# Weight buffers at multiples of 512 bytes, and the first modulation's weights loaded in two halves of the columns

## The chip, the cores and the metric

One core of a Trainium2 chip runs one program. The metric is the device time of one execution in microseconds; for the kernel before it is the median of three runs. The engines are called by the profile's names: PE is TensorE, DVE VectorE, ACT ScalarE, POOL GpSimd, and SP the engine that issues most DMAs. Each runs its own instructions in order.

## The reference

Two layers of a transformer-like block over 256 latent tokens (`x`) and 256 context tokens (`ctx`), width 1024, all in float32. A layer begins with an adaptive norm, whose shift and scale come from a conditioning vector (`c` for the latents, `c_ctx` for the context) through a 1024 x 6144 matrix:

```python
sh1, sc1, g1, sh2, sc2, g2 = split(silu(c) @ w_mod[l] + b_mod[l], 6)
h = layer_norm0(x) * (1.0 + sc1) + sh1
z = h @ w_in + b_in
```

From `z` three mixers are computed (grouped-query attention, a gated linear attention, a neighbourhood attention), gated, summed and projected; then a norm, a second modulation, and a mixture of 32 experts (the top group, then two experts in it), each expert with three matrices of 1024 x 512 (6.3 MB together). The result is the latent stream after two layers.

## The kernel before, in words

`run` (L1645) does, for each layer: the first modulation and norm, the gated linear attention (`gla_gates`, `gla_pair`), attention, neighbourhood attention, merge, output norm, routing, and the experts. Instructions are written in that order and a scheduler places them, by a simulated time line, into each engine's in-order stream; a DMA that is written to `nc.sync` stands in SP's queue, one written to `nc.scalar` in ACT's.

**The start of layer 0.** `setup` (L413) loads the constants (L434). `run` loads four tiles of x, 128 tokens x 1024 columns, 512 KB each, on SP (L1659). `vectors(0)` (L570) loads five small tensors (`bt`, `qk`, `cs`, `wg`, `gn`) and computes the twelve products of the rope table and a few scaled copies on DVE; `setup2` (L441) loads and casts two masks by way of `raw` tiles. Then comes `modulation(0, [0], ...)` (L471): it loads `cT` (L476), computes its SiLU into `sT`, and loads the columns of shift and scale (2048 of the 6144) in 16 tiles `wmod` of 128 x 1024, for each of eight k tiles the two halves of the columns (L493). For every k tile four matmuls with `sT` (32 columns wide, in four column groups of TensorE) add to one PSUM tile, 128 x 512 (L495); an fp32 matmul is two instructions in the profile. So no column is complete until the sixteenth tile has come. The bias `bm` is added (L500), four transposes (L503) and four copies (L517) make `mT`, which holds shift and scale with the feature on the partition. Twelve of the sixteen tiles take buffers of tags that are free at the time (`h4`, `y4`); the last four take the four buffers of tag `raw`, which the first projection weights use next.

**`norm_T`** (L532) computes the statistics of the four x tiles on DVE and the normalised tiles `xh` on ACT (L549). Then come eight parts, (kk, s) for kk = 0 to 3 and s = 0, 1: a part is two k tiles (256 features) of 256 tokens. TensorE transposes (L560), DVE (L565) and ACT (L563) scale and shift one k tile each, ACT casts the result to the rounded high half `hThi` (L291) and DVE or POOL, in turns, subtracts for the low half `hTlo` (L292). Projections are three matmuls per k tile (L380 to L382): high by high, low by high, high by low.

**After it** `gla_gates` (L607) loads `wa`, splits it on ACT and DVE, and accumulates `aT` over k = 0 to 7; the bias on ACT, the gate products `z` (L630), and `projT` (L384) follow, each weight piece coming by way of a `raw` tile (512 KB, L373), a cast on ACT and a subtraction on DVE.

**Where the weights lie.** Pools of SBUF are stacked from the left in the order in which they are opened, some from the right. The staging pool `wp` (`raw`, `whi`, `wlo`, `h4`: 18 tiles of 4 KB per partition) begins 128 bytes past a multiple of 512; the pools opened from the left behind it (`mg`, and for the experts `eg`) begin 64 past one, those from the right (`mp`, `pre`, `ep`) 480 past one. Four two-element tiles `sum0` to `sum3` stand in the pool `lp` ahead of `wp` and take 32 bytes each.

**The experts.** `load` hands out the buffers of the expert weights in rotation: six of the left pool (tag `ew`, 8 KB per partition, 1 MB), then spare staging tiles in pairs (two of 4 KB, 512 KB each), then the right pool's (`ewb`, 8 KB, and the one `pre` buffer of layer 0). The loads stand in SP's queue in that order (L1487), so that in the stream a run of left loads, a run of spare ones and a run of right ones take turns.

Of the kernel before, what the change touches and what calls it, by code (L numbers as in the profile page):

```python
# [10 lines left out]
F32 = mybir.dt.float32  # L11
# [4 lines left out]
AF = mybir.ActivationFunctionType  # L16
ALU = mybir.AluOpType
# [4 lines left out]
NL = 2  # L22
NE = 32
EPS = 1e-6
ALPHA = (2 * NL) ** 0.25
BIG = 1.0e30


A_Q, A_K, B_Q, B_K, B_V, B_R, B_A, C_Q, C_K, C_V, GATE = 0, 512, 768, 1024, 1280, 1792, 2304, 2336, 2848, 3360, 3872
# [135 lines left out]
def _layout(inp):  # L165
# [7 lines left out]

    wm = g["w_mod"].reshape(NL, 8, 128, 3, 2, 1024)
    o["wmod"] = np.ascontiguousarray(wm.transpose(0, 3, 1, 4, 2, 5))
    bm = g["b_mod"].reshape(NL, 3, 4, 512)
    bb = np.zeros((NL, 4, 32, 3, 512), f32)
    bb[:, :, 0] = bm.transpose(0, 2, 1, 3)
# [71 lines left out]
class _Prog:  # L250
# [133 lines left out]
    def projT(self, l, n, ntok):  # L384

        hi, lo = self.piece(l, n)
        p = self.ps("pT")
        for k in range(8):
            s = slice(128 * k, 128 * k + 128)
            self.mm3(p[:, :ntok], hi[:, s], lo[:, s], self.hT(0, k)[:, :ntok], self.hT(1, k)[:, :ntok], k == 0, k == 7)  # L390
        return p

    def projM(self, l, names, kper, width, tiles, sub=None):
# [74 lines left out]
        self.tc.cur_priority -= n  # L468


    def modulation(self, l, groups, tag="raw", tag2="b2", ps="mod"):  # L471

        nc = self.nc
        if l == 0 and 0 in groups:
            cT = self.lp.tile([128, 16], F32, name="cT")
            nc.sync.dma_start(cT, self.a["cT"])  # L476
            th = self.small(16)
            nc.scalar.activation(th, cT, AF.Tanh, scale=0.5)
            sil = self.small(16)
            nc.vector.scalar_tensor_tensor(sil, th, 1.0, cT, op0=ALU.add, op1=ALU.mult)  # L480
            self.sT = self.cp.tile([128, 8, 32], F32, name="sT")
            nc.vector.memset(self.sT, 0.0)
            nc.vector.tensor_scalar(self.sT[:, :, 0:2], sil.rearrange("p (k s) -> p k s", s=2), 0.5, None, op0=ALU.mult)
        for g in groups:
            p = self.ps(ps)
            for k in range(8):
# [42 lines left out]
            self.nc.sync.dma_start(r[:, 512 * i:512 * i + 512], self.md[l, g][row:row + 1, :].to_broadcast([128, 512]))  # L529
        return r  # L530

    def norm_T(self, l, xs):  # L532

        nc = self.nc
        xh = []
# [14 lines left out]
                xh.append(h)  # L550
        hs = [self.t([128, 2, 512], "g4", name="h") for _ in range(4)]
        self.hTt = tuple([self.t([128, 2, 512], "h4", F32R, n) for _ in range(4)] for n in ("hThi", "hTlo"))
        parts = [(s, kk) for s in range(2) for kk in range(4)] if l else [(s, kk) for kk in range(4) for s in range(2)]
        for i, (s, kk) in enumerate(parts):
            ss = slice(256 * s, 256 * s + 256)
            p = self.ps("hT").rearrange("p (k t) -> p k t", k=2)
            for k in range(2):
                kt = 2 * kk + k
                for t in range(2):
                    nc.tensor.transpose(p[:, k, 128 * t:128 * t + 128], xh[2 * s + t][:, 128 * kt:128 * kt + 128], self.ident)  # L560
                sc, sh = (self.mT[l][:, j, s, kt:kt + 1] for j in range(2))
                if k:
                    nc.scalar.activation(hs[kk][:, k, ss], p[:, k], AF.Identity, bias=sh, scale=sc)  # L563
                else:
                    nc.vector.tensor_scalar(hs[kk][:, k, ss], p[:, k], sc, sh, op0=ALU.mult, op1=ALU.add)  # L565
            hi, lo = (self.hTt[j][kk][:, :, ss] for j in range(2))
            self.split(hs[kk][:, :, ss], hi, lo, nc.gpsimd if (kk if l else i) % 2 == PP else None)
# [39 lines left out]
    def gla_gates(self, l):  # L607

        nc = self.nc
        raw = self.raw(l)  # L610
        (nc.scalar if l else nc.sync).dma_start(raw[:, :256], self.a["wa"][l])
        hi, lo = self.t([128, 1024], "whi", F32R), self.t([128, 1024], "wlo", F32R)
        self.split(raw[:, :256], hi[:, :256], lo[:, :256])
        p = self.ps("aT")
        for k in range(8):
            s = slice(32 * k, 32 * k + 32)
            self.mm3(p[:32, :], hi[:, s], lo[:, s], self.hT(0, k), self.hT(1, k), k == 0, k == 7)
        aT = self.t([33, 512], "u2", name="aT")
        nc.scalar.activation(aT[0:32], p[:32], AF.Identity, bias=self.bt[0:32, BT["a"]:BT["a"] + 1])
        nc.vector.memset(aT[32:33], 1.0)  # L620
        self.aT = aT
# [1022 lines left out]
    def run(self):  # L1644
        nc, a = self.nc, self.a  # L1645
        self.md, self.mT, self.mT2, self.nraw = {}, {}, {}, {}
        self.setup()
        self.rp = self.ctx.enter_context(self.tc.tile_pool(name="rp", bufs=1))
        self.x2 = [self.dr.tile([128, 1024], F32, name=f"x2_{t}") for t in range(2)]
        src = [a["x"][0:128], a["x"][128:256], a["cx"][0:128], a["cx"][128:256]]  # L1650
        xs = None
        for l in range(NL):
            T = 4 if l == 0 else 2
            if l == 0:
                left, right = self.mixers(0)
                xs = []
                for t in range(4):
                    x = self.t([128, 1024], "o4", name="x")
                    nc.sync.dma_start(x, src[t])  # L1659
                    xs.append(x)  # L1660
                self.vectors(l)
                self.setup2()
                self.modulation(0, [0], ["h4"] * 8 + ["y4"] * 4 + ["raw"] * 4)
            self.norm_T(l, xs)
            if l:
                self.modulation(1, [1], "o4", "b2", "tmod")
            if l:
# [30 lines left out]
            right.close()  # L1698
            right = self.open("ep", "right", [("ewb", RNG[l]), ("e8", 2), ("g2", T // 2), ("oh", 1), ("o1", 1), ("e2", NE2[l]), *([("c2", NC2[l])] if l else []), ("ct", NCT[l]), ("row", 2)])

            self.sums = [self.cp1(f"sum{t}", 2) for t in range(T)]
            self.experts(l, T)
            if l:
                lgb = self.final_loads(l)
# [38 lines left out]
```

## Time and profile before

| | us |
|---|---|
| median of 3 runs | 2134.95 (2132.41 to 2136.12) |
| profiled execution | 2129.76 |
| its span | 2128.0 |

The span is the time from the first to the last instruction of the profiled execution; what lies around it is 1.76 us. Times in the rows below are microseconds from the span's start. A timeline row is: start, duration, engine, line, operation, tile written <- tiles read, with the idle time of the engine ahead of it and what ended that in brackets; "x4" merges four of a kind. PEclk is the share of TensorE's clock that was granted, DMA share the busy share of the core's 16 DMA engines.

### The profile page before, as it was taken

Reading aid. Unit: us, or ns where it says so; the run is one execution under the profiler, and the core shown is the slowest. Engines: PE = TensorE matmul, PEld = TensorE weight load, DVE = VectorE, ACT = ScalarE, POOL = GpSimd, SP = SyncE. Lnnn points to the kernel's source line nnn. Section 1 sums busy time; section 2 is a strip of 40 time slices with the busy share of each in tenths; the row PEclk is TensorE's granted clock in tenths of the full one; section 3 lists DMA queues with packets and bytes.
Section 4 is the critical chain, followed back from the end, with each engine's and each line's share of the span. In section 5 each row is a group of like instructions: output and inputs, shape, how many; then the busy total and the mean of one; then the engine's idle time right before and its main releaser. Section 6 shows DMA issues by size and latency. Waiting matters only on the chain. (4 is left out here: it accounts for less than half of the span.)

```text
span 2128.0 us, 28181 instructions
## 1 busy us (share of the span) xinstructions
PE 1964.5 (92%) x10749; PEld 1183.4 (56%) x10749; DVE 956.0 (45%) x2275; ACT 569.4 (27%) x1008; POOL 259.9 (12%) x259
## 2 busy tenths in 40 slices
PE   5999999999998998999899698999996999999986
PEld 1676777777885352545253275977895443343332
DVE  4676766464387130222122765776557122222113
ACT  3443344343233000000000454444452101100001
POOL 1322100011110010111011122100020000000000
PEclk9999999999999999999999898999997999999998
DMA  7436222223329899999998734533476999999996
GB/s 294 159 132 218 75 68 73 95 85 103 123 79 380 348 420 419 403 406 419 419 402 339 283 95 138 182 109 102 130 232 268 408 416 418 418 416 419 416 418 245
DMA packets 116435, 562.40 MB, mean 264 GB/s; under 512 B 13575, under 2 KB 15111, under 8 KB 76745
## 3 DMA queue, kind: packets, MB, share of 16 engines
q1 hardware_dynamic: 115720, 558.85, 68.1%
q8 instruction: 87, 1.43, 0.3%
q10 hardware_dynamic: 576, 1.70, 0.2%
q14 instruction: 52, 0.42, 0.1%
HBM read 557.36 MB, written 3.15 MB: 263 GB/s over the span
## 5 line engine op out<-in xcount | busy, mean ns | idle before, releaser
L1525 PE MATMUL h<-ew,XT 128*64 128x512 f32 (+2 forms) x2048 | 478.3, 613 | 29.1 <-DMA ew<-in_ew_dram 29.0
L1525 PEld LDWEIGHTS h<-ew,XT 128*64 128x64 f32 (+2 forms) x2048 | 150.0, 135 | 311.9 <-issue 250.5
L1425 PE MATMUL Y<-ew,aT 128*64 128x512 f32 (+2 forms) x1024 | 250.5, 597 | 11.3 <-DMA ew<-in_ew_dram 6.1
L292 DVE TENSOR_TENSOR wlo<-raw,whi 128x1024 fp32r<-128x1024 f32 (+1 forms) x140 | 179.0, 1279 | 133.6 <-ACT whi L291 132.6
L1447 POOL TENSOR_TENSOR x<-x,ct 128x512 f32<-128x512 f32 x76 | 96.5, 1298 | 933.2 <-DVE ct L1442 636.8
L380 PE MATMUL pT<-hThi,whi 128*128 128x512 f32 (+1 forms) x576 | 203.6, 353 | 2.2 <-DVE zq L880 1.4
L291 ACT CAST whi<-raw 128x1024 fp32r<-128x1024 f32 (+1 forms) x140 | 145.4, 1039 | 224.9 <-PE pT L381 126.8
L382 PE MATMUL pT<-hThi,wlo 128*128 128x512 f32 (+1 forms) x576 | 202.5, 352 | 0.2 <-DVE wlo L292 0.2
L381 PE MATMUL pT<-hTlo,whi 128*128 128x512 f32 (+1 forms) x576 | 202.2, 351 | 0.0
L1415 DVE SCALAR_TENSOR_TENSOR act<-h,s,act 128x512 f32<-128x512 f32 x30 | 22.5, 750 | 317.5 <-PE h L1525 273.8
L1425 PEld LDWEIGHTS Y<-ew,aT 128*64 128x64 f32 (+2 forms) x1024 | 77.5, 133 | 148.5 <-issue 119.7
L818 DVE TENSOR_TENSOR Yl<-Y,Yh 128x512 fp32r<-128x512 f32 x60 | 41.5, 691 | 261.5 <-ACT Yh L817 259.7
L817 ACT CAST Yh<-Y 128x512 fp32r<-128x512 f32 x60 | 35.2, 586 | 420.0 <-PE Y L1425 413.9
L380 PEld LDWEIGHTS pT<-hThi,whi 128*128 128x128 f32 x576 | 110.0, 191 | 22.9 <-ACT whi L291 4.5
L382 PEld LDWEIGHTS pT<-hThi,wlo 128*128 128x128 f32 x576 | 109.8, 191 | 16.3 <-issue 2.6
L381 PEld LDWEIGHTS pT<-hTlo,whi 128*128 128x128 f32 x576 | 110.1, 191 | 14.4 <-issue 1.9
L380 PE MATMUL pM<-whi,hThi 128*128 128x512 f32 (+1 forms) x304 | 110.4, 370 | 2.1 <-DVE zkv L858 1.7
L381 PE MATMUL pM<-wlo,hThi 128*128 128x512 f32 (+1 forms) x304 | 111.4, 367 | 0.0
L382 PE MATMUL pM<-whi,hTlo 128*128 128x512 f32 (+1 forms) x304 | 111.1, 366 | 0.0
L495 PE MATMUL mod<-wmod,sT 128*32 128x512 f32 x320 | 73.9, 625 | 22.2 <-DVE s L343 14.5
L1419 ACT COPY aT<-aT 128x512 f32<-128x512 f32 x30 | 17.6, 586 | 283.8 <-PE aT L1418 283.8
L1395 PE MATMUL XT<-OH,h2hi 128*128 128x256 f32 x352 | 88.9, 290 | 0.0
(373 smaller groups left out, 3084.9 us busy)
## 6 DMA issues: line engine op xcount, KB each, us to landing
ew<-in_ew_dram SPq DMA_DIRECT2D x309, 1024.0 KB, 16.2
ew<-in_ew_dram SPq DMA_DIRECT2D x150, 512.0 KB, 13.8
raw<-in_w_dram SPq DMA_DIRECT2D x145, 512.0 KB, 3.7
wmod<-in_wmod_dram SPq DMA_DIRECT2D x96, 512.0 KB, 6.2
nb<-in_nb_dram SPq DMA_DIRECT2D x32, 256.0 KB, 3.8
g<-md SPq DMA_DIRECT2D x12, 256.0 KB, 11.2
row<-in_ln_dram SPq DMA_DIRECT2D x4, 512.0 KB, 5.2
lgb<-in_ln_dram SPq DMA_DIRECT2D x4, 512.0 KB, 7.8
```

The lines of the kernel that those rows point to most:

```text
L291: self.nc.scalar.copy(hi, src)
L292: (eng or self.nc.vector).tensor_tensor(lo, src, hi.bitcast(F32), op=ALU.subtract)
L380: mm(out, lh, rh, start=start, stop=False)
L381: mm(out, lh, rl, start=False, stop=False)
L382: mm(out, ll, rh, start=False, stop=stop)
L495: nc.tensor.matmul(p[32 * j:32 * j + 32, :], self.sT[:, k, :], raws[j // 2][:, 512 * (j % 2):512 * (j % 2) + 512], start=k == 0, stop=k == 7)
L817: self.nc.scalar.copy(hi, src)
L818: self.nc.vector.tensor_tensor(lo, src, hi.bitcast(F32), op=ALU.subtract)
L1395: mm(p[:, w * j:w * j + w], self.h2s[t][part][:, 128 * k:128 * k + 128], OH[:, t], start=t == 0 and part == 0, stop=t == T - 1 and part == 1)
L1425: mm(y[m * i:m * i + m, :], aT[:, 128 * f + m * i:128 * f + m * i + m], w2(f, n, i), start=f == 0, stop=f == 3)
L1447: nc.gpsimd.tensor_tensor(self.x1[t][:, ns], self.x1[t][:, ns], tmp, op=ALU.add)
L1525: mm(h[m * i:m * i + m, :], XTs[dp][:, k, 128 * pr + m * i:128 * pr + m * i + m], w[i, 2 * q + k // 4][k % 4], start=k == 0, stop=k == 7)
```

## The change

It has two parts that touch each other only in `run`.

The first modulation of layer 0 gets a function of its own, `modulation0`. The same 16 tiles are loaded, but from an array in which the first eight hold, for all eight k tiles, the first 256 columns of each 512, and the second eight the rest. So after eight tiles half of the columns of shift and of scale are complete: those of the k tiles 0, 1, 4 and 5. `half(0)` does matmuls of 256 columns in the four column groups, the add, two transposes and four copies for them; `half(1)` the same for the others. `norm_T` takes its parts in the order kk = 0, 2, 1, 3 and calls the second half after four of the eight parts; a copy of one element from the fourth part's result into the second half's PSUM tile keeps its matmuls behind that. `projT` and `gla_gates` of layer 0 take the k tiles in the same order. The second half's tiles use `y4` and `o4` buffers, so `raw` is left to the projections. The four x tiles and `bm` are issued on ACT's queue, and `vectors` and `setup2` are written behind `norm_T`.

The other part moves addresses: the sums go from four tiles in `lp` to one tile of 64 bytes in `rp`, and a tile of 480 bytes is put at the right edge. `wp`, the left pools and the right pools then all begin at multiples of 512.

```diff
+KK = 0, 2, 1, 3
+KO = [2 * kk + k for kk in KK for k in range(2)], list(range(8))
...
+    w0 = g["w_mod"].reshape(NL, 8, 128, 3, 4, 2, 256)[0, :, :, 0]
+    o["wmod0"] = np.ascontiguousarray(w0.transpose(3, 0, 1, 2, 4)).reshape(2, 8, 128, 1024)
...
-        for k in range(8):
+        for i, k in enumerate(KO[l]):
...
+    def modulation0(self):
...
+        nc.scalar.dma_start(bm, self.a["bmod"][0, :, 0])
+        mT = self.mT[0] = self.lp.tile([128, 2, 2, 8], F32, name="mT0", tag="mT")
+        tags = [["h4"] * 8, ["y4"] * 4 + ["o4"] * 4]
+        raws = []
+        for h in range(2):
+            for k in range(8):
+                raw = self.t([128, 1024], tags[h][k], name="wmod")
+                nc.sync.dma_start(raw, self.a["wmod0"][h, k])
+                raws.append(raw)
+
+        def half(h, after=None):
+            p, pt = self.ps("mod"), self.ps("modT")
+            if after is not None:
+
+                nc.vector.tensor_copy(p[0:32, 0:1], after[0:32, 0:1])
+            for k in range(8):
+                for j in range(4):
+                    nc.tensor.matmul(p[32 * j:32 * j + 32, :256], self.sT[:, k, :], raws[8 * h + k][:, 256 * j:256 * j + 256], start=k == 0, stop=k == 7)
+            hs = slice(256 * h, 256 * h + 256)
+            nc.vector.tensor_tensor(mg[:, hs], p[:, :256], bm[:, hs], op=ALU.add)
+            for q in range(2):
+                nc.tensor.transpose(pt[:, 128 * q:128 * q + 128], mg[:, 256 * h + 128 * q:256 * h + 128 * q + 128], self.ident)
...
+        half(0)
+        return lambda after: half(1, after)
...
-        parts = [(s, kk) for s in range(2) for kk in range(4)] if l else [(s, kk) for kk in range(4) for s in range(2)]
+        parts = [(s, kk) for s in range(2) for kk in range(4)] if l else [(s, kk) for kk in KK for s in range(2)]
         for i, (s, kk) in enumerate(parts):
+            if second and i == 4:
+                second(hs[2][:, 1, 256:257])
...
+        edge = self.ctx.enter_context(self.tc.tile_pool(name="edge", bufs=1, side="right")).tile([128, 120], F32, name="edge")
+        nc.vector.memset(edge, 0.0)
...
-                    nc.sync.dma_start(x, src[t])
+                    nc.scalar.dma_start(x, src[t])
                     xs.append(x)
+                second = self.modulation0()
+                self.norm_T(l, xs, second)
                 self.vectors(l)
                 self.setup2()
-                self.modulation(0, [0], ["h4"] * 8 + ["y4"] * 4 + ["raw"] * 4)
-            self.norm_T(l, xs)
+            else:
+                self.norm_T(l, xs)
...
-            self.sums = [self.cp1(f"sum{t}", 2) for t in range(T)]
+            sums = self.rp.tile([128, 16], F32, name=f"sums{l}", tag="sums")
+            self.sums = [sums[:, 2 * t:2 * t + 2] for t in range(T)]
```

## Rows read from the trace of the kernel before

**Rows 1.** The page's first line.

```profile
span 2128.0 us, 28181 instructions
```

**Rows 2.** Stretches: length, busy us of each engine, PEclk, DMA share, GB/s.

```profile
150.00:480.00 330.00, 321.23 (x1872) 238.19 (x1872) 204.50 (x491) 132.62 (x282) 39.37 (x43) 0.99 0.31 99
1700.00:1900.00 200.00, 197.31 (x928) 82.42 (x928) 49.54 (x81) 21.23 (x37) 20.50 (x16) 1.00 1.02 417
```

**Rows 3.** Timeline of SP's queue: start, us, instruction, tile.

```profile
3.37 0.67 SPq L573 DMA_DIRECT2D bt<-in_bt_dram  x1
...
10.24 0.33 SPq L476 DMA_DIRECT2D cT<-in_cT_dram  x1
...
10.62 13.32 SPq L493 DMA_DIRECT2D wmod<-in_wmod_dram  x16
```

**Rows 4.** Stretches of the start.

```profile
2.00:9.00 7.00, 0.00 (x0) 0.00 (x0) 2.96 (x8) 0.03 (x1) 0.00 (x0) 1.00 0.96 345
9.00:13.00 4.00, 0.00 (x0) 0.00 (x0) 4.00 (x22) 0.21 (x1) 0.00 (x0) 1.00 0.77 216
15.10:33.10 18.00, 15.50 (x60) 2.11 (x56) 1.11 (x10) 4.63 (x4) 0.00 (x0) 1.00 1.02 410
```

**Rows 5.** Timeline of all engines, 33 to 50 us.

```profile
33.83 1.05 PE L495 MATMUL mod<-wmod,sT 128*32 128x512 f32 x4 [0.23 <-DMA wmod<-in_wmod_dram]
...
35.00 0.69 DVE L500 TENSOR_TENSOR mg<-mod,bm 128x512 f32<-128x512 f32 x1 [18.68 <-PE mod L495]
...
35.74 0.65 PE L503 MATMUL modT<-cst,mg 128*128 128x128 f32 x4 [0.86 <-DVE mg L500]
...
36.44 0.39 DVE L517 TENSOR_SCALAR mT<-modT 128x8 f32<-128x8 f32 x4 [0.41 <-PE modT L503]
36.86 1.00 DVE L565 TENSOR_SCALAR h<-hT,mT 128x256 f32<-128x256 f32 x2
...
46.87 0.99 DVE L292 TENSOR_TENSOR hTlo<-h,hThi 128x512 fp32r<-128x512 f32 x1 [0.72 <-ACT hThi L291]
...
49.03 0.40 PE L382 MATMUL aT<-hThi,wlo 128*32 128x512 f32 x1
```

**Rows 6.** Timeline of all engines, 11 to 21 us.

```profile
11.06 0.69 DVE L336 BATCH_NORM_STATS2 s<-x 128x6 f32<-128x512 f32 x1
...
15.63 4.63 ACT L549 ACTIVATE xh<-x,s 128x1024 f32<-128x1024 f32 x4 [3.27 <-DVE s L346]
```

**Rows 7.** Groups by form, TensorE, 640 to 1180 us: busy, mean ns.

```profile
L1425 PE MATMUL Y<-ew,aT 128*32 128x512 f32 x256 | 36.6, 596 | 3.1 <-DVE Yl L818 1.7 <-ACT aT L1419 1.3
```

**Rows 8.** Groups, ScalarE, 36 to 48 us.

```profile
L291 ACT CAST hThi<-h 128x512 fp32r<-128x512 f32 x8 | 4.7, 625 | 0.0
L563 ACT ACTIVATE h<-hT,mT 128x256 f32<-128x256 f32 x8 | 4.2, 571 | 0.0
L291 ACT CAST whi<-raw 128x1024 fp32r<-128x1024 f32 x2 | 2.1, 1046 | 1.6 <-DMA raw<-in_w_dram 1.6
```

**Rows 9.** One stretch at the start of `projT`.

```profile
52.66:56.07 3.41, 3.41 (x9) 2.48 (x9) 0.00 (x0) 2.99 (x4) 0.00 (x0) 0.50 0.90 335
```

**Rows 10.** Groups by form, VectorE, 10 to 15 us.

```profile
L594 DVE TENSOR_TENSOR rope<-cs,qk 128x32 f32<-128x32 f32 x8 | 1.1, 185 | 0.0
L589 DVE TENSOR_TENSOR rope<-cs,qk 128x64 f32<-128x64 f32 x4 | 0.9, 218 | 0.0
```

**Rows 11.** Stretches: left loads, then staging, then right.

```profile
1809.00:1818.50 9.50, 9.50 (x48) 3.26 (x46) 0.00 (x0) 1.08 (x2) 0.00 (x0) 1.00 1.01 419
1823.00:1830.00 7.00, 7.00 (x47) 5.13 (x45) 3.17 (x5) 1.76 (x3) 2.53 (x2) 1.00 1.03 409
1834.50:1841.50 7.00, 7.00 (x29) 2.45 (x27) 4.16 (x6) 0.00 (x0) 2.55 (x2) 1.00 1.01 419
```

**Rows 12.** DMA issues: count, KB each, us to landing.

```profile
ew<-in_ew_dram SPq DMA_DIRECT2D x309, 1024.0 KB, 16.2
ew<-in_ew_dram SPq DMA_DIRECT2D x150, 512.0 KB, 13.8
```

More of the change, by code (lines that the diff above doesn't have):

```diff
@@ L387, in projT @@
         p = self.ps("pT")
-        for k in range(8):
+        for i, k in enumerate(KO[l]):
             s = slice(128 * k, 128 * k + 128)
-            self.mm3(p[:, :ntok], hi[:, s], lo[:, s], self.hT(0, k)[:, :ntok], self.hT(1, k)[:, :ntok], k == 0, k == 7)
+            self.mm3(p[:, :ntok], hi[:, s], lo[:, s], self.hT(0, k)[:, :ntok], self.hT(1, k)[:, :ntok], i == 0, i == 7)
         return p
@@ L468, in later @@
         self.tc.cur_priority -= n
+    def modulation0(self):
+        nc = self.nc
+        cT = self.lp.tile([128, 16], F32, name="cT")
+        nc.sync.dma_start(cT, self.a["cT"])
+        th = self.small(16)
+        nc.scalar.activation(th, cT, AF.Tanh, scale=0.5)
+        sil = self.small(16)
+        nc.vector.scalar_tensor_tensor(sil, th, 1.0, cT, op0=ALU.add, op1=ALU.mult)
+        self.sT = self.cp.tile([128, 8, 32], F32, name="sT")
+        nc.vector.memset(self.sT, 0.0)
+        nc.vector.tensor_scalar(self.sT[:, :, 0:2], sil.rearrange("p (k s) -> p k s", s=2), 0.5, None, op0=ALU.mult)
+        bm = self.t([128, 512], "b2", name="bm")
+        mg = self.t([128, 512], "b2", name="mg")
+        nc.scalar.dma_start(bm, self.a["bmod"][0, :, 0])
[18 more added lines that the diff above has]
+                nc.tensor.transpose(pt[:, 128 * q:128 * q + 128], mg[:, 256 * h + 128 * q:256 * h + 128 * q + 128], self.ident)
+            pv = pt[:, :256].rearrange("p (q r s) -> p r s q", r=4, s=32)
+            for j in range(4):
+                i = 4 * (j % 2) + 2 * h
+                nc.vector.tensor_scalar(mT[:, 1 - j // 2, :, i:i + 2], pv[:, j, 0:2], float(j // 2), None, op0=ALU.add)
+        half(0)
+        return lambda after: half(1, after)
@@ L471, in modulation @@
     def modulation(self, l, groups, tag="raw", tag2="b2", ps="mod"):
         nc = self.nc
[L474 to L483, printed above, removed]
@@ L530, in mod_row, with norm_T @@
         return r
-    def norm_T(self, l, xs):
+    def norm_T(self, l, xs, second=None):
         nc = self.nc
@@ L614, in gla_gates @@
         p = self.ps("aT")
-        for k in range(8):
+        for i, k in enumerate(KO[l]):
             s = slice(32 * k, 32 * k + 32)
-            self.mm3(p[:32, :], hi[:, s], lo[:, s], self.hT(0, k), self.hT(1, k), k == 0, k == 7)
+            self.mm3(p[:32, :], hi[:, s], lo[:, s], self.hT(0, k), self.hT(1, k), i == 0, i == 7)
         aT = self.t([33, 512], "u2", name="aT")
```

## The prediction

> **What bounds the kernel now.** I read the page first: one core, a span of 2128.0 us [rows 1]. Then a table of stretches. In the middle of a layer TensorE is busy 321.23 of 330 us while the DMA engines work a third of the time; in the expert stage the DMA share is 1.02 at 417 GB/s [rows 2]. So the kernel is chained work bound by TensorE, then streams bound by DMA, and the expert stream can begin only when the layer's earlier work has let its buffers go. Whatever the start of the kernel loses or wins is therefore handed on to the end nearly whole; and whatever changes the rate of the expert stream counts at once.
>
> The start is a third kind of stage: nothing runs on TensorE until the first modulation's weights come. In SP's queue the 16 weight loads stand behind the constants, the four x tiles and seven small loads: `bt` is issued at 3.37, `cT` at 10.24, the first weight load at 10.62 [rows 3]. The DMA engines move 345 GB/s in 2 to 9 us, fall to 216 in 9 to 13, and reach 410 only with the weights [rows 4]. The last weights' matmuls start at 33.83; then follow the add, the transposes, the four copies into `mT`, and only at 36.86 the first of eight parts of `norm_T`. Its last low half ends at 47.86 (46.87 + 0.99), the last `aT` matmul at 49.43 [rows 5]. This chain is what the change works on.
>
> **The change part by part.** The profiled execution took 2129.76 us for its span of 2128.0; the median of the runs shown is 2134.95, 0.24% above. I sum against the profiled start-up and take the result off the median.
>
> (a) *The stream ends earlier.* The small loads move behind the weights and x moves to ACT's queue. Bytes up to the last weight: constants 0.315 MB, x 2.097, weights 8.389 and `bm` 0.262 (now ahead, on ACT's queue), 11.06 MB. I let the first 9 us run as before (7 us x 345 = 2.42 MB); the other 8.64 MB at 410 take 21.1 us: 30.1. The same reckoning for before (11.41 MB, with 0.86 MB in 9 to 13) gives 32.8, so the gain is **-2.7 us**, and the last weights' matmuls start at 31.1. Bounds: 345 GB/s until x and as many bytes of weights are in gives -1.7; 410 from 2 us on gives -3.8.
>
> The x tiles get later: with the two queues sharing, x and as many bytes of weights are in at 9 + (0.315 + 4.19 - 2.42)/0.41 = 14.1, where the last statistics started at 11.06. Those took until 15.63 to release the first of four scalings of 1.16 us [rows 6]. Moved by 3 us, the last ends at some 22 to 23, and with fewer operations on VectorE at 20.5. The first half's weights are in at about 20.2, its `mT` at 22.9. The x tiles thus cost nothing, covered by 2 us; a slower x queue would be late next.
>
> (b) *From the last weights to `mT`.* Before: 33.83 to 36.86, 3.03 us [rows 5]. After: a load of 128x1024 holds four column groups of 256 instead of two of 512. The nearest row is the four-group matmul of the experts, 256 instructions in 36.6 us [rows 7]: eight instructions, four groups of 512 columns, take 1.14, so 256 columns 0.6. The add over 256 columns lies between 0.35 and 0.69 (I take 0.4); two transposes of the four, 0.4; the copies 0.39; gaps 0.25. Sum 2.0: **-1.0** (0 to -1.2). The first part of the second half then starts at 33.1.
>
> (c) *Only four parts of eight stay behind it.* In 36.86 to 47.86 ScalarE has eight scalings of 0.571, eight casts of 0.625 and two weight casts of 1.046 [rows 8]; the parts follow each other at about 1.0 us there. Four parts and the last low half: 5.1 us instead of 11.0, **-5.9** if nothing else sits between them. The other four lie at about 23 to 28, beside the loads.
>
> (d) *The second half's matmuls.* The one-element copy holds them until the fourth part's scaling, about 22.9 + 3.2 = 26.1; behind them in TensorE's order stand the transposes of the other four parts. Eight loads x 0.6 = 4.8 bring them to 30.9, even with the stream. At half clock they need 9.6, to 35.7, 4.0 us late. The clock does fall after a thin stretch: it is 0.50, 1.2 GHz, in 52.66 to 56.07, after TensorE had had only two gate products since 49.43 [rows 9], and the second half too follows a stretch of transposes alone. Between 0 and +4.0 I take **+0.8**.
>
> (e) *What moves into the remaining parts.* The small loads (0.61 MB) now land at 31 to 33 and `wa` and the first weight piece behind them, at some 33.5 and 35. On VectorE the twelve rope products (1.1 + 0.9 us [rows 10]) and the other copies of these loads, 3.2 us in all, stood in its wait for weights; they can now stand between the parts. On ScalarE up to two weight casts (2.1 [rows 8]) and a wait for `wa` can. Nothing of it is needed before `aT`: between 0 and +3.2, I take **+1.5**.
>
> (f) *At nothing:* the edge's memset runs while VectorE waits for the first x; the sums stay on one engine; the order 0, 2, 1, 3 of the k tiles issues the same matmuls. The `bm` load and four issues of x move to ACT's queue, which has only an activation table to load before 12 us.
>
> (g) *Addresses.* Weight buffers begin now at 128 (staging), 64 (left) and 480 (right) past a multiple of 512, afterwards at 0. I placed windows in runs of loads of one kind, by their order in the queue: left 419 GB/s, right 419, staging 409 [rows 11]. The first two have 8 KB per partition, the third 4 KB. On one of 16 engines that is 312.8 ns for 8 KB and 160.2 for 4 KB, so 7.6 ns of each run don't depend on its length. Offsets of 64 and 480 give the same rate, so where a run starts hasn't shown; no row has one at 0. Bounds: all 7.6 ns of the 309 + 150 expert loads [rows 12] (8 runs per engine each, 3672) would be 28 us won; a loss of the same kind has no row that excludes it. I take **0**, as the two offsets that can be compared do.
>
> By the Trainium skill ("DMA: Bandwidth & Descriptors", How a descriptor splits into AXI transactions) a run is cut at multiples of 256 bytes, and one that starts off such a multiple costs extra 32-byte beats; by it the sum would fall further, as the second rival below has it, and the equal rates of left and right speak against it.
>
> Sum: -2.7 - 1.0 - 5.9 + 0.8 + 1.5 = **-7.3 us**, 2127.6. With the bounds of (a) to (e): -10.9 to -0.4.
>
> **The rivals.**
> 1. *The start is eaten up* (0.14). The second half at half clock, (d) at +4.0, or ScalarE's in-order wait for `wa` in (e) at +3.2: the sum is -4.1 by the first alone and -2.4 by both, 2132.5. For it: the clock row. Against: at full clock the matmuls keep pace with the loads, and `wa` lands about when the second half's first part starts.
> 2. *Aligned runs are cheaper* (0.18). Half of the 7.6 ns gone is 14 us of expert stream: 2113.6; all of it 2099.6. Within it (0.05) stands a mechanism of beats: a run pays for the bytes between the 256 boundary below and its start, 2 beats of 32 bytes at 64, 4 at 128, 7 at 480. A beat is 1.19 ns ((312.8 - 160.2)/128). By the rotation of buffers 180 of the 1 MB loads go left, 129 right, and I count the 150 half loads as staging: 8 x (360 + 903 + 600) x 1.19 ns = 17.7 us, 2109.9. Against it: right would be 6 ns a run, 8 GB/s, slower than left, and rows 11 have 419 for both. The skill's section named above is this rule.
> 3. *Aligned buffers stream slower* (0.12). If equal starting phases of all buffers make transfers or engines meet, it strikes the expert stream: 309 x 2.50 + 150 x 1.28 = 965 us. It decides against the gain from 7.3/965, 0.76%: 419 falling to 415.8. At 409, the lowest rate of rows 11, the 8 KB loads alone cost 18.9: 2146.5. For it: nothing but that no row has offset 0. Against: the two offsets seen don't differ.
>
> **How the numbers follow.** Forecast 0.56, rivals 0.14, 0.18, 0.12. What a measurement tells from no change is 0.2%, 4.3 us. Forecast and rival 2 are faster: 0.74; rival 1 is within it: 0.14; rival 3 slower: 0.12. The forecast's own range is 2124.1 to 2130.7. For 8 in 10 I take rival 1 and the start of both others: below to 2110, which leaves out the larger half of rival 2 (0.09); above to 2141, which leaves out 0.09 of rival 3.
>
> **What would show it.** First weight load issued before 3 us; last weights' matmuls near 31; four of eight parts before 28; last `aT` matmul near 42 instead of 49.43; the same distances from there on; 419 and 409 GB/s unchanged in the same runs of loads. Wrong if the streams leave 415 to 423, if `aT` ends after 45, or if the second half's matmuls start after 28 or run at half clock.

## The result, and the profile after

The kernel after takes 2110.1 us, the median of four runs (2108.23 to 2114.3), against 2133.68 of the kernel before on the same chip (2130.98 to 2136.12). The ratio is 0.9893, 95% interval 0.9872 to 0.9913; by the ratio that is 22.8 us less, and between 18.6 and 27.3. The profiled execution took 2108.9 us for a span of 2107.0.

The page of the kernel after, the row of the DMA rate in 40 slices of 52.7 us:

```profile
GB/s 309 146 136 222 73 70 72 96 93 103 118 80 384 352 426 426 391 406 426 426 402 356 286 96 147 181 106 111 127 228 253 414 423 425 425 424 426 423 425 242
```

Stretches of the kernel after (columns as in rows 2): the expert stream, three of the start, and three at half clock.

```profile
1700.00:1900.00 200.00, 196.60 (x917) 79.82 (x917) 48.39 (x79) 20.67 (x36) 20.29 (x16) 1.00 1.02 425
2.00:9.00 7.00, 0.14 (x4) 0.17 (x8) 3.19 (x11) 1.50 (x2) 0.00 (x0) 1.00 0.95 373
9.00:13.00 4.00, 2.02 (x16) 0.26 (x14) 3.69 (x16) 0.56 (x1) 0.00 (x0) 1.00 1.04 420
15.10:28.00 12.90, 9.15 (x62) 4.52 (x59) 4.66 (x18) 5.99 (x10) 1.33 (x2) 1.00 1.03 421
28.40:31.80 3.40, 3.40 (x40) 1.69 (x36) 2.71 (x12) 0.00 (x0) 0.81 (x1) 0.50 1.12 312
38.70:42.10 3.40, 3.40 (x10) 1.60 (x11) 2.53 (x3) 2.48 (x6) 2.34 (x2) 0.51 1.05 341
48.90:55.70 6.80, 6.80 (x13) 3.64 (x12) 0.29 (x2) 4.18 (x5) 0.32 (x1) 0.50 0.65 234
```

The expert stream runs at 425 GB/s where [rows 2] have 417, with the DMA share as full as before, and in both layers (the slices of 423 to 426). At the start the DMA engines move 373, 420 and 421 GB/s where [rows 4] have 345, 216 and 410. But TensorE, busy all through the last three stretches, is granted half its clock there, 1.2 of 2.4 GHz: 13.6 us in which it does the work of 6.8.

The timeline of the kernel after, the second half of the modulation and what follows:

```profile
27.92 5.35 PE L509 MATMUL mod<-wmod,sT 128*32 128x256 f32 x64 [2.54 <-DVE mod L506]
...
33.57 0.40 ACT L298 CAST whi<-raw 128x256 fp32r<-128x256 f32 x1 [5.19 <-DMA raw<-in_wa_dram]
34.00 0.43 DVE L299 TENSOR_TENSOR wlo<-raw,whi 128x256 fp32r<-128x256 f32 x1 [0.40 <-ACT whi L298]
34.34 0.42 DVE L511 TENSOR_TENSOR mg<-mod,bm 128x256 f32<-128x256 f32 x1
34.87 1.05 ACT L298 CAST whi<-raw 128x1024 fp32r<-128x1024 f32 x1 [0.90 <-DMA raw<-in_w_dram]
...
35.35 0.37 DVE L517 TENSOR_SCALAR mT<-modT 128x4 f32<-128x4 f32 x4 [0.59 <-PE modT L513]
35.95 1.23 DVE L299 TENSOR_TENSOR wlo<-raw,whi 128x1024 fp32r<-128x1024 f32 x1 [0.22 <-ACT whi L298]
37.09 1.90 DVE L608 TENSOR_SCALAR h<-hT,mT 128x256 f32<-128x256 f32 x4
...
37.20 1.05 ACT L298 CAST whi<-raw 128x1024 fp32r<-128x1024 f32 x1 [1.29 <-DMA raw<-in_w_dram]
...
38.16 1.02 ACT L606 ACTIVATE h<-hT,mT 128x256 f32<-128x256 f32 x2
...
44.90 0.69 DVE L299 TENSOR_TENSOR hTlo<-h,hThi 128x512 fp32r<-128x512 f32 x1 [3.10 <-ACT hThi L298]
...
46.67 0.39 PE L389 MATMUL aT<-hThi,wlo 128*32 128x512 f32 x1
...
48.55 3.48 PE L673 MATMUL z<-aT,wg 33*128 33x512 f32 x4 [1.49 <-ACT aT L662]
...
51.95 0.80 PE L387 MATMUL pT<-hThi,whi 128*128 128x512 f32 x1
```

These lines answer to [rows 5]. The second half's 64 matmuls take 5.35 us, partly at half clock. The add into `mg` stands behind `wlo` of `wa`, which waits for a cast on ScalarE that waited 5.19 us for its DMA. Then two weight casts stand on ScalarE (34.87 and 37.20, each after a wait for its DMA) and one `wlo` on VectorE (35.95) ahead of the first scalings of the second half. The last `aT` matmul ends at 47.06, 2.4 us earlier than in [rows 5], and the gate products `z` run at half clock: `projT` starts at 51.95, where before it started at 52.9.

So of the 22.8 us only one is won where the start hands over to `projT`. The table follows the rest through the kernel: us from the span's start, read from the timelines, and in brackets what has been won by then. The last two columns are the two parts of the change alone (the experiments below); "halves" stands for the whole first part, the moved loads included. Each column is one execution, and that of the addresses alone is the fastest of its five (2111.86, median 2117.22), so its column shows some 5 us more than the median won.

```
                           before    after           addresses only   halves only
last aT matmul, layer 0      49.4    47.1 (-2.4)      49.7 (+0.2)      48.7 (-0.7)
projT starts, layer 0        52.9    52.0 (-1.0)      53.1 (+0.1)      52.7 (-0.2)
attention starts, layer 0   238.7   233.5 (-5.2)     236.8 (-2.0)     236.2 (-2.5)
first expert, layer 0       691.6   684.5 (-7.1)     686.7 (-4.9)     690.2 (-1.4)
experts end, layer 0       1178.4  1167.5 (-10.9)   1169.7 (-8.7)    1175.1 (-3.3)
last aT matmul, layer 1    1225.1  1213.5 (-11.6)   1216.4 (-8.7)    1222.6 (-2.5)
modulation, layer 1        1306.3  1290.7 (-15.5)   1297.6 (-8.7)    1299.9 (-6.4)
first expert, layer 1      1649.7  1635.7 (-14.0)   1639.4 (-10.3)   1643.2 (-6.5)
experts end, layer 1       2113.0  2092.2 (-20.8)   2095.1 (-17.8)   2106.5 (-6.5)
```

Two kinds of stage give. Where weights stream, the addresses give, most in the experts of layer 1 (7.5 us of the 17.8). And two stretches between, which no line of the change touches, are shorter in the kernel after: from `projT` to the attention of layer 0 by 4.2 us, of which each part of the change alone has about half (2.1 and 2.3), and from the last `aT` matmul to the modulation in layer 1, its gated linear attention, by 3.9 us, which of the two parts only the halves have.

### The profile page after: what moved, and what is told of

Same layout as the page of the kernel before. It is cut to its first block, busy times and chain, and to the rows that moved or that the text cites. A ratio compares the mean times of both kernels' runs of the same rounds, so it can differ in the third digit from the quotient of the medians.

```text
span 2107.0 us, 28317 instructions
## 1 busy us (share of the span) xinstructions
PE 1955.0 (93%) x10813; PEld 1184.1 (56%) x10813; DVE 960.2 (46%) x2282; ACT 568.9 (27%) x1008; POOL 258.2 (12%) x259
## 5 line engine op out<-in xcount | busy, mean ns | idle before, releaser
L1438 PE MATMUL XT<-OH,h2lo 128*128 128x256 f32 x352 | 86.9, 285 | 0.0
```

Of the source, the lines that this page charges most:

```text
L1438: mm(p[:, w * j:w * j + w], self.h2s[t][part][:, 128 * k:128 * k + 128], OH[:, t], start=t == 0 and part == 0, stop=t == T - 1 and part == 1)
```

## The experiments

My theory after the result: the addresses carry most of the gain, because a run of bytes that begins at a multiple of 256 or 512 costs less; the halves give their part, but not at the start. Rival: the halves carry it, and the higher rate of the stream is a by-product that hides behind TensorE.

**The two parts, one at a time.** `e1_halves` is the kernel after without the tile at the edge and with the four old tiles of sums; `e2_align` is the kernel before with those two edits alone.

```diff
 e1_halves (against the kernel after)
-        edge = ... .tile([128, 120], F32, name="edge")
-        nc.vector.memset(edge, 0.0)
...
-            sums = self.rp.tile([128, 16], F32, name=f"sums{l}", tag="sums")
-            self.sums = [sums[:, 2 * t:2 * t + 2] for t in range(T)]
+            self.sums = [self.cp1(f"sum{t}", 2) for t in range(T)]
 e2_align (against the kernel before): the same lines, + and - exchanged
```

> The two halves of the first modulation alone, every weight buffer where it was before (128, 64 and 480 bytes past a multiple of 512). Theory (addresses carry the gain, the start gives back nearly all of its own): 0 to 6 us below the kernel before, expert streams at 417 to 419 GB/s as before, projT starting at 51 to 53 us. Rival (the start carries the gain, the faster stream is a side show): 10 us or more below the kernel before.

> The addresses alone (edge tile, sums moved), the first modulation as before. Theory: 14 to 20 us below the kernel before, 8 KB loads of the experts at 425 to 426 GB/s and the 4 KB ones above 415, projT starting at 52 to 53 us as before. Rival: within 5 us of the kernel before.

Measured: the halves alone 2123.49 us, ratio 0.9962 (0.9948 to 0.9975); the addresses alone 2117.22, ratio 0.9936 (0.9923 to 0.995). Against 2131.86 of the kernel before beside them that is 8.1 (5.3 to 11.1) and 13.6 us (10.7 to 16.4), and the two add up to 21.7 of the 22.8. The 8.1 lie between the theory's 0 to 6 and the rival's 10, the 13.6 just under the 14 to 20 expected. The expert stream of layer 1, halves alone:

```profile
1700.00:1900.00 200.00, 197.27 (x926) 80.79 (x924) 49.00 (x79) 20.70 (x36) 20.36 (x16) 1.00 1.02 417
```

and addresses alone:

```profile
1700.00:1900.00 200.00, 196.79 (x926) 80.83 (x922) 48.66 (x79) 21.22 (x37) 20.47 (x16) 1.00 1.02 424
```

The rate is 417 with the old addresses and 424 with the new, whatever the start does. On TensorE, ScalarE, GpSimd and SP the kernel with new addresses alone issues the same instructions in the same order as before (but for two neighbouring pairs of matmuls), and VectorE has only the memset of the edge and the sums' new tile. Nor is it TensorE's clock: runs with the same mean granted clock, 0.971 to 0.972, take 2116.29 to 2120.7 us with the new addresses and 2131.68 to 2132.86 before. What is left to make the difference is where the buffers lie.

**Which addresses.** `e3_at256` is the kernel after with every weight buffer moved by 256 bytes: 256 past a multiple of 512.

```diff
-        edge = ... .tile([128, 120], F32, name="edge")
+        edge = ... .tile([128, 56], F32, name="edge")
...
+        pad = self.lp.tile([128, 64], F32, name="pad")
+        nc.vector.memset(pad, 0.0)
```

> The changed kernel with every weight buffer moved by 256 bytes, so at 256 past a multiple of 512. If multiples of 256 are what counts: as the changed kernel, 425 GB/s in the expert streams. If it takes multiples of 512: 418 GB/s, and some 14 us slower than the changed kernel. A third outcome, a rate between them, would say that the loss grows with the offset.

Measured: 2108.79 us, ratio 0.9886 (0.9871 to 0.9901), and 425 GB/s in the same stretch of the expert stream. What counts is a multiple of 256, not of 512.

`m1_offsets` measures the price by itself, in one execution. Fourteen phases of 24 loads of 1 MB (8 KB per partition) or 32 of 512 KB (4 KB) go into 16 buffers, each phase at one offset from a multiple of 512. All of the reference's computation is left out.

```diff
+PHASES = [(0, 2048), (64, 2048), (128, 2048), (256, 2048), (480, 2048), (32, 2048), (4, 2048), (0, 2048),
+          (0, 1024), (64, 1024), (128, 1024), (256, 1024), (480, 1024), (0, 1024)]
...
+            s = (off - 128) % 512 // 4
+            x = big[n % 16][:, s:s + w]
+            nc.sync.dma_start(x, ew[0, n % 32][:, n // 32 % 6, :w])
```

> Nothing but expert loads in a stream, no other engine at work, in phases whose destinations start 0, 64, 128, 256, 480, 32, 4 and 0 bytes past a multiple of 512, first with 8 KB per partition, then with 4 KB. It leaves out the whole computation and stores loaded weights. If the loss belongs to the transfer itself: 425 GB/s at 0, 417 to 419 at every other offset (or at those that are no multiple of 256), and the same order with 4 KB. If it comes from engines that read SBUF at the same time: one rate for all offsets.

Stretches of that kernel, each inside one phase, in the order of the list (length, POOL, PEclk, DMA share, GB/s):

```profile
10.00:58.00 48.00, 0.00 (x0) 1.00 1.01 428
65.00:118.00 53.00, 0.00 (x0) 1.00 1.01 422
...
185.00:236.00 51.00, 0.00 (x0) 1.00 1.01 428
244.00:296.00 52.00, 0.00 (x0) 1.00 1.01 421
303.00:356.00 53.00, 0.00 (x0) 1.00 1.01 420
363.00:416.00 53.00, 0.00 (x0) 1.00 1.01 419
423.00:475.00 52.00, 0.00 (x0) 1.00 1.01 427
482.00:515.00 33.00, 0.00 (x0) 1.00 1.03 420
522.00:556.00 34.00, 0.00 (x0) 1.00 1.03 410
563.00:597.00 34.00, 0.00 (x0) 1.00 1.03 410
604.00:637.00 33.00, 0.00 (x0) 1.00 1.03 420
644.00:678.00 34.00, 0.00 (x0) 1.00 1.03 409
```

(Left out are 128 with 8 KB, 422, and the last phase, offset 0 with 4 KB again, 420.) With 8 KB a start at 0 or 256 moves 427 to 428 GB/s and every other start 419 to 422; with 4 KB it is 420 against 409 to 410. No engine computes here, so the loss is the transfer's own. Worked out per run of bytes on one of 16 engines, 64 costs 131072/422 - 131072/427.5 = 4.0 ns, 480 costs 4.7, and 128 with 4 KB 65536/410 - 65536/420 = 3.8. For the expert loads, with the counts that the prediction used, that is 8 x (180 x 4.0 + 129 x 4.7 + 150 x 3.8) = 15 us, an estimate for both layers that stands beside the 13.6 measured (10.7 to 16.4); the two expert stages of the table got 3.8 and 7.5 us shorter.

The price does not grow with the distance: 480 bytes past a multiple of 512 cost 4.7 ns, 32 cost 5.5 and 4 cost 6.2. The Trainium skill ("DMA: Bandwidth & Descriptors", How a descriptor splits into AXI transactions) cuts a run at multiples of 256 bytes, and that boundary is borne out, 256 being as good as 0. Its count of beats, which grows with the bytes between the boundary and the start, is not: by it 480 would cost seven times 32, and the rows have 421 and 420.

**Where the start loses its gain: loads alone.** `e8_moved` is the kernel with the new addresses, x on ScalarE's queue and the small loads behind the weights, but the first modulation whole and all eight parts of `norm_T` behind it.

```diff
 against the kernel before; the edge and the sums as in e2_align
...
-                    nc.sync.dma_start(x, src[t])
+                    nc.scalar.dma_start(x, src[t])
                     xs.append(x)
+                self.modulation(0, [0], ["h4"] * 8 + ["y4"] * 4 + ["o4"] * 4)
+            self.norm_T(l, xs)
+            if l == 0:
                 self.vectors(l)
                 self.setup2()
-                self.modulation(0, [0], ["h4"] * 8 + ["y4"] * 4 + ["raw"] * 4)
-            self.norm_T(l, xs)
```

> The kernel before with the new addresses and with the loads in the new order (x on ScalarE's queue, the small loads behind the weights), but the first modulation whole and all eight parts behind it. Theory (the halves bring little where the attention begins, because the start is eaten up): the last weights' matmuls at 30 to 31 instead of 33.8, the last `aT` matmul ends at 46.5 to 47.5, as in the kernel after, and the time lies within 3 us of the kernel after's, ratio 0.989 to 0.9915. Rival (it is the halves that bring the 7 us between the aligned kernel and the kernel after): `aT` ends at 47 or later, `projT` starts after 52.5 and the ratio stays at 0.992 to 0.9945, as with the addresses alone. If the order of layer 1's linear attention stays that of before, the 81 us from its `aT` to its modulation stay too; if it becomes that of the halves, they fall to 77.

Measured: ratio 0.9922 (0.99 to 0.9944). Its timeline, the last weights' matmuls and `mT`, and one stretch:

```profile
29.13 1.05 PE L495 MATMUL mod<-wmod,sT 128*32 128x512 f32 x4 [0.18 <-DMA wmod<-in_wmod_dram]
...
32.93 0.37 DVE L517 TENSOR_SCALAR mT<-modT 128x8 f32<-128x8 f32 x4
...
35.90:46.10 10.20, 8.80 (x28) 5.00 (x29) 7.24 (x9) 8.79 (x18) 4.17 (x4) 0.50 0.71 238
```

Against [rows 5] the last weights' matmuls start 4.7 us earlier and `mT` 3.5, and yet the last `aT` matmul ends at 49.5 instead of 49.4, and `projT` starts at 52.9 as before. My theory expected 46.5 to 47.5 and missed; the rival's 47 or later, 52.5 or later and 0.992 to 0.9945 came true. But the interval reaches into that of the kernel after, so what the halves add to the moved loads, some 6 us by the two ratios, is not shown. At the start an earlier stream was worth nothing by itself. Part of what ate it is the clock: TensorE is granted half of it in 35.9 to 46.1, where the kernel before has all of it (1.00 in 36 to 52); the `aT` matmuls there follow each other in 0.43 us, behind it in 0.23.

**What the parts wait for: four runs that missed.** `e4_between` issues the small loads between the two halves, so that `wa` and the weight pieces land earlier. `e5_busy` puts filler matmuls into the thin stretches to keep TensorE's clock, `e6_both` does both. `e7_ahead` issues `wa` and the first two weight pieces ahead of the small loads.

```diff
 e4_between
             for h in range(2):
+                if h and between is not None:
+                    between()
...
-                second = self.modulation0()
+                second = self.modulation0(lambda: (self.vectors(0), self.setup2()))
                 self.norm_T(l, xs, second)
-                self.vectors(l)
-                self.setup2()
 e5_busy
+    def busy(self, x, n):
+        p = self.ps("busy")
+        for _ in range(n):
+            self.nc.tensor.matmul(p[:, :256], x, self.c["iota"], start=True, stop=True)
...
+            self.busy(mg[:, 256 * h:256 * h + 128], (4, 6)[h])
...
+            if l == 0 and i < 6:
+                self.busy(hs[kk][:, 0, 256 * s:256 * s + 128], 2 if i < 4 else 1)
 e7_ahead
+                for n in (None, ("Bq", 0), ("Bk", 0)):
+                    raw = self.raw(l)
...
+                    self.ahead.append(raw)
                 self.norm_T(l, xs, second)
```

> The changed kernel with the small loads (rope, biases, masks) issued between the two halves of the weights instead of behind both; nothing else. Theory (the second half's gain went into in-order waits of ScalarE and VectorE for the first projection weights, which land behind the small loads): the casts of those weights no longer wait, the first scaling of the second half on ScalarE at 35 to 36 us instead of 38.2, the last aT matmul at 44 to 45 instead of 47.1, projT 2 to 3 us earlier; the second half's weights land 1.5 to 2 us later without costing anything. Rival (TensorE's clock alone ate it): aT ends at 46.5 or later.

> The changed kernel with 20 fp32 matmuls of 256 columns put between the transposes of the start, into a PSUM tile that nobody reads, so that TensorE is not idle there. Theory of the clock: no stretch at half clock between 26 and 34 us, the second half's matmuls end at 31.5 to 32 instead of 33.3, the gates' at full clock. Theory of the in-order waits: ScalarE still waits for the weights until 37 to 38, so that aT ends at 45 to 47, at most 2 us earlier than in the changed kernel.

> Both edits together: small loads between the halves, and the extra matmuls. If the two causes add: aT ends at 42 to 43.5 us, projT starts at 45 to 47, and 3 to 5 us less than the changed kernel where the first expert matmul starts. If only one of them is real, no better than the better of the two alone.

> The kernel after, with `wa` and the first two weight pieces issued right behind the 16 weight loads, ahead of the seven small loads. Theory (ScalarE's in-order waits for weight pieces that land behind the small loads delay the second half's parts): `wa` is there before the second half's matmuls end, the first scaling of the second half starts at 36 instead of 38.2, the last `aT` matmul ends at 44 to 45 instead of 47.1 and `projT` starts at 49 to 50 instead of 52.0; the time is 0 to 2 us below the kernel after's, ratio 0.988 to 0.990. Rival (the half clock sets the start): the first scaling is earlier but the transposes, `aT` and the gate products run longer at half clock, and `projT` starts at 51.5 or later.

Measured, ratio with its interval, last `aT` matmul, start of `projT` (the kernel after: 0.9893, 47.1, 52.0):

```
e4_between   0.9902  0.9874 to 0.993    46.2   49.6
e5_busy      0.9917  0.9888 to 0.9946   49.0   52.4
e6_both      0.9939  0.9923 to 0.9954   50.2   53.6
e7_ahead     0.9917  0.9895 to 0.9939   49.0   54.1
```

These places are one execution each, and they move by more than the orders of instructions explain. Up to the attention `e3_at256` issues the same instructions in the same order as the kernel after, apart from the memset of its pad; yet its last `aT` matmul ends at 46.3 and its `projT` starts 2.2 us earlier:

```profile
49.71 0.50 PE L387 MATMUL pT<-hThi,whi 128*128 128x512 f32 x1
```

Its half clock lies in other places, so that its gate products take 1.98 us instead of 3.48: from 26.9, 37.1 and 50.8, 3.4 us each, where the kernel after has it from 28.4, 38.7 and 48.9 (3.4, 3.4 and 6.8). So `e4_between` has won nothing that `e3_at256` has not.

The fillers did what they were for: in `e5_busy` 28.4 to 31.8 is granted the full clock and the second half's matmuls take 3.66 us instead of 5.35,

```profile
31.18 3.66 PE L514 MATMUL mod<-wmod,sT 128*32 128x256 f32 x64
...
35.72 2.75 PE L481 MATMUL busy<-cst,mg 128*128 128x256 f32 x12
```

but they start 3.3 us later, and the fillers at 35.72 take 2.75 us ahead of the next transposes. The last `aT` matmul ended at 49.0, not at the 45 to 47 expected: the half clock costs less than keeping the clock up in this way. `e4_between` came to 46.2 where 44 to 45 were expected: two weight casts still stood ahead of the first scaling, at 37.44. `e6_both`, expected at 42 to 43.5, pays for its fillers as `e5_busy` does. `e7_ahead` ends where its rival, the half clock, had it (`projT` at 54.1), but not by the rival's way: the first scaling came not earlier but later, at 40.54. It shows another obstacle. Its VectorE:

```profile
34.25 1.23 DVE L299 TENSOR_TENSOR wlo<-raw,whi 128x1024 fp32r<-128x1024 f32 x1 [3.17 <-ACT whi L298]
...
35.48 0.42 DVE L514 TENSOR_TENSOR mg<-mod,bm 128x256 f32<-128x256 f32 x1
...
36.72 1.22 DVE L299 TENSOR_TENSOR wlo<-raw,whi 128x1024 fp32r<-128x1024 f32 x1
...
38.57 0.36 DVE L520 TENSOR_SCALAR mT<-modT 128x4 f32<-128x4 f32 x4
```

The second half's matmuls had ended at 32.45 (27.49 + 4.96). The add into `mg` came 3 us later, and `mT` after another 3, because subtractions for weight pieces that nobody needs before `projT` stood ahead in VectorE's order. Written earlier, the pieces were merely scheduled earlier, into the very chain that they were to help.

**The place of the casts.** `e9_hold` is the kernel after with one thing held back: a copy of one element from the last part's result into the high half of the first three weight pieces, so that neither their casts nor their subtractions can go ahead of the parts. `e10_hold_between` is the same on `e4_between`.

```diff
         hi, lo = self.t([128, 1024], tags[0], F32R), self.t([128, 1024], tags[1], F32R)
+        if l == 0 and self.nraw[l] <= 4:
+            nc.scalar.copy(hi[0:32, 0:1], self.hlast)
         self.split(raw, hi, lo)
...
+        self.hlast = hs[3][0:32, 1, 256:257]
```

> The kernel after, with a copy of one element from the last part's result into the high half of the first three weight pieces, so that their casts and subtractions can't stand ahead of the second half's parts. Theory (what eats the start is the in-order place of casts and subtractions of weight pieces that land late and aren't needed yet): the first scaling of the second half on ScalarE starts at 36.0 to 36.5 instead of 38.16, the last `aT` matmul ends at 43 to 45 instead of 47.1, `projT` starts at 47.5 to 50 instead of 52.0; 1 to 4 us less than the kernel after, ratio 0.987 to 0.989. Rival (the start is bound by the half clock and the transposes' order): `aT` ends at 46 or later, and the casts behind it now delay `projT`, which starts at 52 or later; ratio 0.989 to 0.991.

> The same hold, with the small loads between the two halves as in e4_between. Theory: the first scaling at 36.0 instead of that run's 37.44, `aT` ends at 43.5 to 45 instead of 46.2, `projT` starts at 47.5 to 49 instead of 49.6; ratio 0.987 to 0.989. Rival: no earlier than e4_between, `aT` at 46 or later, `projT` at 49.5 or later.

The timeline of `e9_hold`, the same places as in the timeline after:

```profile
34.23 0.42 DVE L513 TENSOR_TENSOR mg<-mod,bm 128x256 f32<-128x256 f32 x1
...
35.24 0.37 DVE L519 TENSOR_SCALAR mT<-modT 128x4 f32<-128x4 f32 x4 [0.59 <-PE modT L515]
35.65 1.90 DVE L611 TENSOR_SCALAR h<-hT,mT 128x256 f32<-128x256 f32 x4
...
36.72 1.02 ACT L609 ACTIVATE h<-hT,mT 128x256 f32<-128x256 f32 x2 [2.87 <-PE hT L606]
...
41.87 0.69 DVE L299 TENSOR_TENSOR hTlo<-h,hThi 128x512 fp32r<-128x512 f32 x1 [1.70 <-ACT hThi L298]
...
41.96 2.00 ACT L298 CAST whi<-raw 128x1024 fp32r<-128x1024 f32 x2
...
44.80 1.98 PE L676 MATMUL z<-aT,wg 33*128 33x512 f32 x4 [0.77 <-ACT aT L665]
...
46.71 0.50 PE L389 MATMUL pT<-hThi,whi 128*128 128x512 f32 x1
```

and two of its stretches, which in the kernel after were at half clock:

```profile
38.70:42.10 3.40, 3.40 (x17) 1.54 (x14) 1.15 (x2) 2.49 (x8) 2.43 (x2) 1.00 0.58 229
48.90:55.70 6.80, 6.80 (x32) 5.63 (x31) 4.79 (x14) 3.26 (x4) 0.83 (x1) 1.00 0.67 254
```

`mT` is there when it was (35.24), but VectorE's first part follows at once instead of behind a `wlo`, ScalarE's at 36.72 instead of 38.16 (0.2 later than expected), and the casts come at 41.96. The last low half ends at 42.6 instead of 45.6, the last `aT` matmul at 44.0 (43 to 45 expected), `projT` starts at 46.71, earlier than the 47.5 to 50 expected, with TensorE at the full clock in both stretches. That the closer chain kept the clock up is not shown: a spell of 6.8 us at half clock comes at 110.2 instead, and in `e3_at256` spells moved without any change of order. At the last `aT` matmul and at `projT` the start is 3.0 and 5.2 us ahead of the kernel after, 2.3 and 3.0 ahead of `e3_at256`. The time is 2103.63 us (2102.31 to 2106.53), but beside a kernel before of 2130.04; the ratio, 0.9883 (0.9866 to 0.9899), hardly differs from those of the kernel after (0.9893) and `e3_at256` (0.9886). So the place where the start gains is shown, and a gain of the whole kernel over the kernel after is not. `e10_hold_between` has 2103.67, ratio 0.9876 (0.986 to 0.9893), `aT` at 44.9 and `projT` at 47.6 as expected, but its first scaling at 37.60 instead of 36.0: the two edits don't add.

**The stretches that no line touches.** No run was made for them, but the traces of the others can be compared. The table has their length, how much of it the granted clock was half, and whether VectorE and ScalarE issue the instructions in the order of before or in a new one:

```
               projT to attention, layer 0         last aT matmul to modulation, layer 1
               us     at half clock   order        us    at half clock   order
before        185.8       10.0        old         81.2       13.7        old
e2_align      183.7        3.4        old         81.2       13.7        old
e8_moved      186.2       10.2        a third     78.8       13.7        new
e3_at256      184.3       10.2        new         78.8       13.7        new
e1_halves     183.5        9.0        new         77.3       10.2        new
after         181.6        3.8        new         77.3       10.2        new
```

How the order differs in layer 1 is seen in the ten us that begin 70 behind the last `aT` matmul, of the kernel before, the kernel after and `e8_moved`:

```profile
1295.10:1305.10 10.00, 10.00 (x53) 8.83 (x52) 4.91 (x26) 1.00 (x5) 0.00 (x0) 0.83 0.15 53
...
1283.50:1293.50 10.00, 9.16 (x62) 6.73 (x60) 8.95 (x29) 3.56 (x8) 3.08 (x4) 1.00 0.27 66
...
1289.30:1299.30 10.00, 10.00 (x70) 8.22 (x72) 8.71 (x36) 3.70 (x10) 1.93 (x2) 1.00 0.13 53
```

VectorE does 4.91 us of work before and 8.95 after. The scheduler, which places every instruction by a simulated time line, has put the same source into another order. `e8_moved` has that order too, with the modulation whole: it does not take the halves, the moved loads and the lines moved with them bring it. At equal half clock (13.7 us) the new order is 2.4 us shorter in layer 1, and at 10.0 and 10.2 it is 1.5 shorter in layer 0; within one order the kernel after is 2.7 us shorter than `e3_at256` in layer 0 with 6.4 us less at half clock, and 1.5 shorter in layer 1 with 3.5 less. So order and clock share the two stretches. These are one trace per kernel, and why the half clock falls in one trace and not in another is open.

## Why the prediction was right and wrong

The forecast was 2127.6 with a range from 2110 to 2141; 2110.1 lies at its lower edge, where the second rival was let in. Faster was right, but that the time lies inside the range, by 0.1 us, is luck: what the forecast put the gain down to carried only a third of it (8.1 of 22.8), and even that, close to the 7.3 forecast, was not won where it was expected.

**(g) is the step that failed.** I took 0, "as the two offsets that can be compared do". The comparison was sound and beside the point: 64 and 480 are both off a multiple of 256, and all off starts cost about the same, so equal rates of left and right said nothing about a start at 0. The right number stood in the bounds: of the 7.6 ns per run that don't depend on its length, half or a little more, 3.8 to 4.7 at the offsets of this kernel, is the price of the start. That is the second rival's main case (14 us, 2113.6), which I gave 0.18. Its mechanism of beats, 2109.9, comes nearest to the time and is the wrong one: `m1_offsets` has no growth with the offset. The third rival is refuted, no phase at 0 is slower than one off a multiple of 256.

**(a)** was under-sized: `e8_moved`, where nothing holds the last weights' matmuls back, has them at 29.13 where I had 31.1, 4.7 us won, beyond the bound of 3.8. The rate is 420 GB/s already in 9 to 13 us, and of the difference half a microsecond is the new addresses' (8.39 MB at 420 instead of 410).

**(c), (d) and (e)** are where the start failed, together by 5 us at the last `aT` matmul (42.1 forecast, 47.06 measured).
- (d) took +0.8 of 0 to +4.0 and measured +2.4: the matmuls ended at 33.27, not at 30.9. They started at 27.92 instead of 26.1, before the clock fell: the first half's `mT` was there at 22.62 (22.25 + 0.37), near the 22.9 forecast, but from it to the second half's matmuls the four parts took 5.3 us and not 3.2. Then the half clock that [rows 9] had shown came here too (0.50 in 28.4 to 31.8), as it is named under what would make the prediction wrong.
- (e) took +1.5 of 0 to +3.2 and named ScalarE's casts and the wait for `wa`. It left out VectorE: the add behind `wlo` of `wa`, and the `wlo` between `mT` and the first part. Four parts took 8.5 us (37.09 to 45.59) and not the 5.1 of (c). `e9_hold` takes the weights' casts and subtractions out and has 6.9 (35.65 to 42.56), at full clock; what keeps these from 5.1 is open.
- The first rival, "the start is eaten up" at 2132.5, had the mechanism at the start right, half clock and in-order waits. That its size is right too (-2.4 by both its terms, and -2.4 at the last `aT` matmul) is partly chance: (d) was +2.4 and not +4.0, (a) was under-sized, and `e3_at256` with the same order has -3.1 there. Its whole time was wrong because of (g).

**"Handed on nearly whole"** can't be read from so small a gain: the 1.0 us at `projT` are less than the place moves by itself (2.2 in `e3_at256`). At `projT` the halves alone had won 0.2 us (1.0 with the addresses), and at the end they were worth 8.1. Most of the rest was won in stretches far behind the change, by another order of instructions there and by less half clock, which I had both set to nothing by "the same distances from there on".

## What to carry to other kernels

Keep the SBUF start of every streamed buffer at a multiple of 256 bytes: pools that began 64, 128 and 480 bytes past a multiple of 512, the staging pool only because four tiles of 32 bytes stood in front of it, cost this DMA-bound stream 1.7% of its rate, and it is mended without touching an instruction of the work. When a load is moved earlier, look up what the in-order engines of the chain will then find ready: casts and subtractions of later weights slip in ahead of the work that the load was moved for, and a dependency of one element holds them back. Before a gain far behind a change is put down to the change, compare the order of instructions and the granted clock there, and a second kernel with the same order. And a rate that is the same at two offsets is no evidence about a third; ask whether any of the rows is of the kind that the change makes.

## What the runs showed of the hardware

A load into SBUF pays some 4 to 6 ns per run of bytes for a start off a multiple of 256, whether 4 bytes off or 224: 1.3 to 2.0% with 8 KB and 2.4 to 2.6% with 4 KB (`m1_offsets`). Some 5.5 ns of a run stay at offset 0 too (2 x 65536/420 - 131072/427.5). And half-clock spells are not bound to the order of instructions: `e3_at256` issues its start in the order of the kernel after and has them from 26.9, 37.1 and 50.8 us instead of from 28.4, 38.7 and 48.9.
